# The last projection pairs product by product, the first scan items moved beside them, and a new order at five seams of a hybrid SSD block

## The chip, the cores and the metric

One Trainium2 chip, one core of it. The metric is the device time of one execution in microseconds; the time before is the median of three runs.

## What is computed

The reference is one pre-norm encoder block on a sequence of 1024 rows of 1024 numbers in float32, with a selective scan (SSD) and a gated short convolution side by side, and a SwiGLU feed-forward part behind them:

```python
h = rmsnorm(x, norm_mix_w)
u = h @ w_in                                  # 1024 x 10272
z, xbc, dt_raw, s_b, s_c, s_x, g_a, g_b = split(u)
xbc = silu(causal_depthwise_conv(xbc, ssd_conv_w) + ssd_conv_b)
y = ssd_chunked_scan(xs, softplus(dt_raw + dt_bias), -exp(a_log), bm, cm)   # 4 groups, 8 heads each
y = group_rmsnorm((y + d_skip * xs) * silu(z)) * ssd_norm_w
branch_a = y @ w_ssd_proj
branch_b = (s_b * causal_depthwise_conv(s_c * s_x, sconv_w)) @ w_sconv_proj
x = x + (sigmoid(g_a) * branch_a + sigmoid(g_b) * branch_b) @ w_o
x = x + (silu(hn @ w_gate) * (hn @ w_up)) @ w_down      # hn = rmsnorm(x, norm_ffn_w)
out = rmsnorm(x, norm_out_w)
```

## The kernel before

Every fp32 operand is split into a high and a low part, and every product is three matmuls (high by high, low by high, high by low; lines 679 to 681, and 81 to 83 for the direct tiles). A matmul is 128 x 128 by 512 columns.

**Projection.** The input projection is worked in *pairs*: two neighbouring tiles of 128 columns of w_in are one Strassen-Winograd step of seven products (class Pair, lines 834 to 908). A *slot* is one product of one pair, 12 matmuls; `slots` lists them in order, and a pair costs 84 matmuls. The first three pairs (`first`) go product by product, all three pairs at each product, so that the halves of the normalised x can be made beside them; the other 27 pairs go one after the other, seven slots each. For each product ScalarE writes the high part of a weight combination (`hi`, line 864), VectorE its low part (`lo`, line 868), and the results are added up on both engines (`ev`). `STAGES` says how many slots ahead of its product each stage is issued. `put` (line 823) splits one x-side operand (T1, T2, T3, B11, B12, B22 ...) into th (ScalarE) and tl (VectorE), line 76 and 77.

**Direct tiles and scans.** Twenty column tiles (`direct`: z tiles 12 to 15, then the 16 gate tiles) are plain products of 48 matmuls each (8 blocks of the inner dimension, two halves, three matmuls). Their weights are prepared one tile ahead (`direct_hi` on ScalarE, `direct_lo` on VectorE). Beside them the scan runs: `scans()` is a generator of 65 steps, and `direct_tile` pumps a step whenever `due` says so, evenly over the tiles. A scan item (one group, one block of 128 rows) has `part1` (transposes and score matmuls on TensorE, the decay matrix by Relu and Exp on ScalarE, the masked scores on VectorE, lines 408 to 457) and `part2` (state and output, lines 459 to 500). `prep2` makes the decay matrix of the item ahead. `norm` (line 502) is the gated group norm of a finished stretch: sums by TensorE, a square root chain of VectorE and ScalarE (lines 99 to 107, tiles gv, gr, gq), a transpose to a row (prt, line 532), a round trip through memory that spreads the row (rs_d, rbc, lines 536 and 538, issued by GpSimd), the scaling (line 543), and the operands of the next stage (line 557, written out at 558). `step_norms` advances every norm that is open, oldest first.

**Behind them** come the merge gemms, the output projection, the feed-forward units and the down projection, all as Strassen steps, with a seam where the feed-forward part gets its operands (`ffn_phase`: `first_half`, `second_half`), and a tail that norms the last rows and writes them.

The program order on every engine is written out by hand; each engine takes its instructions in that order, and a DMA stands in the order of the engine that issues it.

## Time and profile before

| | |
|---|---|
| median of 3 runs | 1910.98 us (1909.13 to 1911.13) |
| the profiled execution's own time | 1910.68 us |
| its span, first to last instruction | 1908.9 us |
| TensorE busy, matmuls | 1879.7 us (98%), 8905 recorded |
| VectorE, ScalarE, GpSimd busy | 68%, 51%, 9% |
| stages by TensorE: x and its norm; first three pairs | to 19.3; to about 76 us |
| 27 pairs | to 618.97 us |
| direct tiles with the scan | to about 952 us |
| merge, output projection, feed-forward, down projection | to 1901.6 us |
| tail | to 1908.9 us |

The profile counts an engine as busy while one of its instructions runs. The matmul records overlap: one is 0.39 us long while the next begins 0.227 us later, so the start-to-start distance is the price of a matmul. A row of the timeline gives start, duration, engine, line, operation and operands; in square brackets stands how long the engine stood idle before and what released it. The view of waits sums those idle times by engine, line and releaser.

### The profile page before, as it was taken

How to read it: one execution, taken by the hardware profiler on the slowest of the kernel's cores; microseconds unless marked ns; L12 is line 12 of the kernel's file. 1: busy time of each engine (PE TensorE's matmuls, PEld its weight loads, DVE VectorE, ACT ScalarE, POOL GpSimd, SP SyncE). 2: the span in 40 equal slices, each digit the busy share in tenths (PEclk: the TensorE clock that was granted, in tenths of full speed). 3: DMA queues.
4: the chain of work that ended last, by engine and by line, in shares of the span. 5: the costliest groups of instructions: out<-in, count | busy, mean ns of one | idle time of the engine just before them, and what ended most of it. 6: DMA issues, size and time to landing. Idle time of an engine off the chain costs nothing.

```text
span 1908.9 us, 24143 instructions
## 1 busy us (share of the span) xinstructions
PE 1879.7 (98%) x8905; PEld 1545.3 (81%) x8905; DVE 1299.4 (68%) x1688; ACT 970.6 (51%) x1541; POOL 169.7 (9%) x196
## 2 busy tenths in 40 slices
PE   7999999999999999999999999999999999999998
PEld 5688888888888888888878888887888888888886
DVE  7667878777785678889878548877444444456465
ACT  5545454444444987877665454464333333345333
POOL 1010111101100000101010000101211121100000
PEclk9999999999999999999999999999999999999999
DMA  5197999978959656778798665917988888867552
GB/s 181 48 275 173 240 230 236 240 187 226 264 149 288 223 194 219 251 250 269 261 321 311 226 208 203 229 80 171 215 193 220 195 193 192 232 257 286 190 196 110
DMA packets 341190, 411.97 MB, mean 216 GB/s; under 512 B 17384, under 2 KB 223936, under 8 KB 341072
## 3 DMA queue, kind: packets, MB, share of 16 engines
q1 hardware_dynamic: 284400, 308.59, 50.0%
q0 software_dynamic: 48608, 72.47, 20.9%
q10 hardware_dynamic: 8064, 29.36, 3.8%
q8 instruction: 70, 1.15, 0.2%
q14 instruction: 48, 0.39, 0.1%
HBM read 320.56 MB, written 143.15 MB: 243 GB/s over the span
## 4 chain that ended last, share of the span: by engine, by line
PE 92%; DVE 4%; ACT 2%; DMA 1%; issue 1%; SPq 0%; ACTq 0%; DVEq 0%
PE pb L679 5%; PE pb L680 5%; PE pb L681 5%; PE gb L679 5%; PE gb L680 5%; PE gb L681 5%; PE fb L681 4%; PE fb L679 4%; PE fb L680 4%; PE pr L81 4%; PE pr L83 4%; PE pr L82 4%; PE gd L679 4%; PE pd L679 4%; PE gd L681 4%; PE gd L680 4%
## 5 line engine op out<-in xcount | busy, mean ns | idle before, releaser
L77 DVE TENSOR_TENSOR wl<-ws,wh 128x1024 fp32r<-128x1024 f32 x77 | 94.0, 1221 | 121.6 <-ACT wh L76 121.6
L679 PE MATMUL gb<-qh,gh 128*128 128x512 f32 x432 | 169.1, 391 | 1.1 <-DVE h L1132 1.1
L680 PE MATMUL gb<-ql,gh 128*128 128x512 f32 x432 | 168.9, 391 | 0.0
L681 PE MATMUL gb<-qh,gl 128*128 128x512 f32 x432 | 168.7, 391 | 0.0
L681 PE MATMUL fb<-th,wl 128*128 128x512 f32 x352 | 137.1, 389 | 0.8 <-DVE wl L77 0.8
L679 PE MATMUL fb<-th,wh 128*128 128x512 f32 x352 | 137.1, 390 | 0.6 <-ACT wh L76 0.6
L680 PE MATMUL fb<-tl,wh 128*128 128x512 f32 x352 | 137.0, 389 | 0.0
L81 PE MATMUL pr<-th,wh 128*128 128x512 f32 x320 | 131.1, 410 | 0.0
L679 PE MATMUL gd<-qh,gh 128*128 128x512 f32 x324 | 126.0, 389 | 0.0
L680 PE MATMUL gd<-ql,gh 128*128 128x512 f32 x324 | 126.0, 389 | 0.0
L681 PE MATMUL gd<-qh,gl 128*128 128x512 f32 x324 | 126.0, 389 | 0.0
L83 PE MATMUL pr<-th,wl 128*128 128x512 f32 x320 | 125.1, 391 | 0.0
L82 PE MATMUL pr<-tl,wh 128*128 128x512 f32 x320 | 124.9, 390 | 0.0
L76 ACT ACTIVATE qh<-cb 128x1024 fp32r<-128x1024 f32 x98 | 99.8, 1018 | 38.0 <-PE gb L680 17.1
L77 DVE TENSOR_TENSOR ql<-cb,qh 128x1024 fp32r<-128x1024 f32 x98 | 115.6, 1180 | 1.6 <-ACT qh L76 1.4
L74 DVE SCALAR_TENSOR_TENSOR gl<-ca,gh 128x1024 fp32r<-128x1024 f32 (+1 forms) x60 | 70.5, 1174 | 49.0 <-ACT gh L73 49.0
L681 PE MATMUL fd<-th,wl 128*128 128x512 f32 x264 | 102.7, 389 | 0.0
L679 PE MATMUL fd<-th,wh 128*128 128x512 f32 x264 | 102.7, 389 | 0.0
L680 PE MATMUL fd<-tl,wh 128*128 128x512 f32 x264 | 102.7, 389 | 0.0
L679 PEld LDWEIGHTS gb<-qh,gh 128*128 128x128 f32 x432 | 81.5, 189 | 18.4 <-DVE h L1132 1.4
L679 PE MATMUL pb<-th,wh 128*128 128x512 f32 x240 | 94.4, 394 | 1.0 <-ACT u L894 1.0
L681 PEld LDWEIGHTS gb<-qh,gl 128*128 128x128 f32 x432 | 81.5, 189 | 17.1
(324 smaller groups left out, 4702.3 us busy)
## 6 DMA issues: line engine op xcount, KB each, us to landing
ws<-in_w_in_dram SPq DMA_DIRECT2D x80, 512.0 KB, 6.3
ws<-in_w_gate_dram SPq DMA_DIRECT2D x77, 256.0 KB, 3.9
ws<-in_w_up_dram SPq DMA_DIRECT2D x77, 256.0 KB, 4.4
ca<-u_d SPq DMA_DIRECT2D x35, 512.0 KB, 5.3
ab<-ac_d SPq DMA_DIRECT2D x32, 512.0 KB, 6.0
xbc_g<-cv ACTq DMA_DIRECT2D x24, 512.0 KB, 7.0
ws<-ws POOLq DMA_DIRECT2D x22, 512.0 KB, 6.4
wd_d<-in_w_down_dram SPq DMA_DIRECT2D x20, 512.0 KB, 10.8
```

The lines of the kernel that those rows point to most:

```text
L74: nc.vector.scalar_tensor_tensor(lo, src, -1.0, hi.bitcast(F32), op0=ALU.mult, op1=ALU.subtract)
L76: nc.scalar.activation(hi, src, AF.Copy)
L77: nc.vector.tensor_sub(lo, src, hi.bitcast(F32))
L81: nc.tensor.matmul(o, lh, rh, start=first, stop=False)
L82: nc.tensor.matmul(o, lh, rl, start=False, stop=False)
L83: nc.tensor.matmul(o, ll, rh, start=False, stop=last)
L679: nc.tensor.matmul(o, lh, rh, start=first, stop=False, skip_group_check=True)
L680: nc.tensor.matmul(o, lh, rl, start=False, stop=False, skip_group_check=True)
L681: nc.tensor.matmul(o, ll, rh, start=False, stop=last, skip_group_check=True)
```

## The change

1. Z tiles 12 to 15 become two more pairs (`z_pairs` up to 16), and `direct` holds the 16 gate tiles only.
2. The last three pairs (three z pairs) are worked product by product: n = 1, 2, 6 for all three, then n = 5 and 3 for each, then 7 for all, then 4 for all. The stage that makes the weights of product 7 is now tied to product 3, which goes before it. Weight loads of these pairs come later and closer together (`load_pairs`).
3. Six scan steps (`EARLY`) are pumped beside the last eleven slots: the loads of the first items with 10 slots left, part1 of the first three items with 6, 5 and 2 left, part2 of the first two with 3 and 0 left. One step was there before, with 2 slots left. The direct tiles pump the other steps, now over 16 tiles.
4. `step_norms` advances the newest norm first.
5. Start of the program: two of the first four x loads and the other four are issued by ScalarE instead of SyncE, the later weight loads of the first pairs by GpSimd. The operand T2 is put one step earlier.
6. Feed-forward seam: ScalarE scales one of four row blocks instead of two, the operand T3 is summed by an accumulating DMA instead of VectorE, and one of the two subtractions of T4 goes a step earlier.
7. Tail: the sum of squares goes to the square root without an add of its own (part of it is known before), and the last row block is written in two halves from two queues.

```diff
         def step_norms():
-            for n in list(norms):
+            for n in norms[::-1]:
...
-    z_pairs = [Pair(i * P, (silu_z(i), silu_z(i + 1))) for i in range(0, 12, 2)]
+    z_pairs = [Pair(i * P, (silu_z(i), silu_z(i + 1))) for i in range(0, 16, 2)]
...
-    NF = len(first)
+    NF, NL = len(first), 3
     slots = [(p, n) for n in (1, 2, 5, 6, 7, 3, 4) for p in first] + \
-        [(p, n) for p in rest_p for n in ORDER]
+        [(p, n) for p in rest_p[:-NL] for n in ORDER] + \
+        [(p, n) for n in (1, 2, 6) for p in rest_p[-NL:]] + \
+        [(p, n) for p in rest_p[-NL:] for n in (5, 3)] + \
+        [(p, n) for n in (7, 4) for p in rest_p[-NL:]]
...
-        for stage, what, d in STAGES[n]:
+        for stage, what, d in STAGES[{7: 3, 3: 7}.get(n, n) if p in rest_p[-NL:] else n]:
...
-    direct = [(wslab(w_in, i * P), z_raw(i)) for i in range(12, 16)]
+    direct = []
     for j in range(KT):
         direct += [(wslab(w_in, GA0 + j * P), gate_raw(ga_d[j])), (wslab(w_in, GB0 + j * P), gate_raw(gb_d[j]))]
...
-                due = turn[0] * SCAN_STEPS // (len(direct) * 2 * KT - 4)
+                due = turn[0] * (SCAN_STEPS - 5) // (len(direct) * 2 * KT - 4)
...
-            rows0 = h1_rows(0, (2, 3))
+            rows0 = h1_rows(0, (3,))
...
             raw0[0].clear()
+            for k in range(2):
+                nc.gpsimd.dma_start(raw1[0][k], raw1[1][k], accum_op=ALU.add)
             every(put("T2", t2))
             yield
             every(put("T1", t1))
             yield
-            for k in range(2):
-                V.tensor_add(raw1[0][k], raw1[1][k], raw1[0][k])
             every(put("T3", raw1[0]))
             yield
+            V.tensor_sub(raw0[1][0], raw0[1][0], t2[0])
             every(put("B22", raw1[1]))
             yield
-            for k in range(2):
-                V.tensor_sub(raw0[1][k], raw0[1][k], t2[k])
+            V.tensor_sub(raw0[1][1], raw0[1][1], t2[1])
             every(put("T4", raw0[1]))
...
-            r = finish(range(t, t + 1))
+            r = rstd2_of(sq[:, t, 0:1], known[:, m:m + 1])
...
-            nc.sync.dma_start(out[t * P:(t + 1) * P, :], fo[t])
+            if m < 3:
+                nc.sync.dma_start(out[t * P:(t + 1) * P, :], fo[t])
+            else:
+                nc.scalar.dma_start(out[t * P:(t + 1) * P, 512:1024], fo[t][:, 512:1024])
+                nc.sync.dma_start(out[t * P:(t + 1) * P, 0:512], fo[t][:, 0:512])
...
-    a0 = rows_sq(xt[0:4], "x", "avav")
+    a0 = rows_acc(xt[0:4], "x")
+    rows_sq_on("a", a0, "x")
+    rows_sq_on("v", a0, "x")
+    rows_sq_on("a", a0, "x")
+    more_loads(4)
+    more_loads(6)
+    small_loads()
+    first[1].y.load(nc.gpsimd)
...
-            yield
-        every(put("T2", t2))
+            if k == 7:
+                every(put("T2", t2))
+            yield
...
+    T_LAST = {12: "T2", 7: "T1", 3: "T3"}
+    EARLY = (10, 6, 5, 3, 2, 0)
...
         if left == 2:
             direct_lo(direct[0][0])
+        if left in EARLY:
             pump_scan()
```

Two places in the program show what this does to the order on the engines.

**The end of the pairs, ScalarE.** Before, from the high part for the last product (wk, its pair's product 4) to the decay matrix of the first scan item (th are the two halves of operand B12, wh a direct tile's weights, u a z tile and its silu):

```order
L864 ACTIVATE wk_4537<-ws_4295 128x512
L76 ACTIVATE th_4539<-br_4442 128x1024
L76 ACTIVATE th_4543<-br_4443 128x1024
L897 ACTIVATE u_4560<-pd_4547 128x512
L987 ACTIVATE wh_4563<-ws_4483 128x1024
L612 ACTIVATE u_4498<-u_4498 128x1024
L613 DMA z_g_120<-u_4498 128x1024
L905 ACTIVATE u_4560<-pb_4485 128x512
L612 ACTIVATE u_4560<-u_4560 128x1024
L613 DMA z_g_120<-u_4560 128x1024
L987 ACTIVATE wh_4630<-ws_4566 128x1024
L398 ACTIVATE ab_4586<-ab_4586,pac 128x128 x8
```

Now, from the silu of the last pair to B12 (the first of the three wk for product 4 stands just ahead of it):

```order
L613 ACTIVATE u_4533<-u_4533 128x1024
L614 DMA z_g_121<-u_4533 128x1024
L399 ACTIVATE ab_4689<-ab_4689,pac 128x128 x8
L401 ACT_TABLE_LOAD
L401 ACTIVATE ab_4689<-ab_4689 128x1024
L437 ACTIVATE bh_4794<-pcb_4790 128x128
```

```order
L401 ACTIVATE ab_4691<-ab_4691 128x1024
L865 ACTIVATE wk_4835<-ws_4333 128x512
L437 ACTIVATE bh_4848<-pcb_4844 128x128
L441 ACTIVATE xw_4851<-xx_4847 128x512
L455 ACTIVATE y_4779<-bc_4685,cols 128x128 x2
L455 ACTIVATE y_4780<-x_598_4687,cols 128x128 x2
L397 ACTIVATE cd_4864<-ab_4783 128x8
L399 ACTIVATE ab_4783<-ab_4783,pac 128x128 x8
L401 ACTIVATE ab_4783<-ab_4783 128x1024
L865 ACTIVATE wk_4889<-ws_4378 128x512
L76 ACTIVATE th_4891<-br_4716 128x1024
L76 ACTIVATE th_4895<-br_4717 128x1024
```

The decay matrix and part1 of the first scan items, which followed all weights of the pairs, now stand between the high parts of products 4 of the second and third pair, and B12 stands behind the last of these.

On VectorE, the same place now (tl is the low part of B12, the last two rows of wk are the low parts for products 4):

```order
L451 TENSOR_TENSOR xw_4851<-xx_4847,xw_4851 128x512
L900 TENSOR_TENSOR u_4709<-u_4709,pb_4505 128x512
L869 TENSOR_TENSOR wk_4835<-ws_4333,wk_4835 128x512
L77 TENSOR_TENSOR tl_4892<-br_4716,th_4891 128x1024
L77 TENSOR_TENSOR tl_4896<-br_4717,th_4895 128x1024
L900 TENSOR_TENSOR u_4749<-u_4749,pb_4520 128x512
L869 TENSOR_TENSOR wk_4889<-ws_4378,wk_4889 128x512
```

The low part for the last product 4 stands behind both tl, which read what ScalarE makes last.

**The last scan norms, GpSimd and VectorE.** GpSimd before, with the row's round trip (rs_d, rbc) of the norm before the last, and the operands yt of the norm before that:

```order
L558 DMA yt_d_162<-s_1240_8139 128x2x512
L558 DMA yt_d_163<-s_1241_8140 128x2x512
L558 DMA yt_d_164<-y_6768 128x2x512
L536 DMA rs_d_137<-rst_8232 4x128
L538 DMA rbc_8235<-rs_d_137 128x512
L558 DMA yt_d_165<-y_6316 128x2x512
```

and now:

```order
L559 DMA yt_d_162<-s_1250_8162 128x2x512
L559 DMA yt_d_163<-s_1251_8163 128x2x512
L537 DMA rs_d_137<-rst_8238 4x128
L539 DMA rbc_8241<-rs_d_137 128x512
L559 DMA yt_d_164<-y_6836 128x2x512
L559 DMA yt_d_165<-y_6405 128x2x512
```

The round trip no longer stands behind the third yt. On VectorE the scaling by rbc and the square root chain of the last norm (gv to gr) stood, before:

```order
L543 SCALAR_TENSOR_TENSOR y_7211<-y_7211,cols,rbc_8235 128x512 x2
L543 SCALAR_TENSOR_TENSOR y_7212<-y_7212,cols,rbc_8235 128x512 x2
L99 TENSOR_SCALAR gv_8383<-pq_8378 128x4
L102 RECIPROCAL gr_8385<-gr_8385 128x4
L104 TENSOR_TENSOR gq_8388<-gr_8385 128x4
```

and now:

```order
L544 SCALAR_TENSOR_TENSOR y_7260<-y_7260,cols,rbc_8241 128x512 x2
L99 TENSOR_SCALAR gv_8388<-pq_8383 128x4
L102 RECIPROCAL gr_8390<-gr_8390 128x4
L104 TENSOR_TENSOR gq_8393<-gr_8390 128x4
L105 TENSOR_TENSOR gq_8393<-gq_8393,gv_8388 128x4
L106 TENSOR_SCALAR gq_8393<-gq_8393 128x4
L107 TENSOR_TENSOR gr_8390<-gr_8390,gq_8393 128x4
L544 SCALAR_TENSOR_TENSOR y_7261<-y_7261,cols,rbc_8241 128x512 x2
```

The chain stands behind half of the scaling instead of all of it.

## Rows read from the trace of the kernel before

**Rows 1.** The page, busy time of TensorE and its share of the span and the other engines beside it.

```profile
PE 1879.7 (98%) x8905; PEld 1545.3 (81%) x8905; DVE 1299.4 (68%) x1688; ACT 970.6 (51%) x1541; POOL 169.7 (9%) x196
```

**Rows 2.** The waits of TensorE over the whole span: line that waited, releaser, us in total, times, longest.

```profile
PE prt L532 <- DVE gr L107: 2.1, 1, 2.1
...
PE gb L679 <- DVE h L1132: 1.1, 1, 1.1
...
PE fb L681 <- DVE wl L77: 0.8, 1, 0.8
PE fb L679 <- ACT wh L76: 0.6, 1, 0.6
```

**Rows 3.** The timeline of TensorE near its end; 13 matmuls begin between the first and the last row.

```profile
1898.27 0.39 PE L680 MATMUL gb<-ql,gh 128*128 128x512 f32 x1
...
1901.22 0.39 PE L681 MATMUL gb<-qh,gl 128*128 128x512 f32 x1
```

**Rows 4.** The timeline of TensorE at the end of the pairs: the first matmul of the first direct tile, part1 of the first scan item from its transposes to the next product, and the score products of a part2.

```profile
618.97 0.39 PE L81 MATMUL pr<-th,wh 128*128 128x512 f32 x1
...
622.37 0.38 PE L426 MATMUL pxt<-ident,bc 128*128 128x128 f32 x2
...
623.06 0.49 PE L81 MATMUL pr<-th,wh 128*128 128x512 f32 x1
...
631.57 1.09 PE L489 MATMUL pdg<-ab,xx 128*64 128x128 f32 x16
```

**Rows 5.** The timeline of ScalarE from the last pair to the second scan item: a high part of a combination, a silu with the DMA issue behind it, B12, the Relu that begins the decay matrix of the first item, and the first and last instruction of part1.

```profile
601.25 0.63 ACT L864 ACTIVATE wk<-s 128x512 fp32r<-128x512 f32 x1 [0.53 <-DVE s L847]
601.79 1.05 ACT L612 ACTIVATE u<-u 128x1024 f32<-128x1024 f32 x1
602.87 0.33 ACTq L613 DMA_DIRECT2D z_g<-u  x1
...
609.51 2.00 ACT L76 ACTIVATE th<-br 128x1024 fp32r<-128x1024 f32 x2
...
622.23 2.43 ACT L398 ACTIVATE ab<-ab,pac 128x128 f32<-128x128 f32 x8
...
626.94 0.26 ACT L436 ACTIVATE bh<-pcb 128x128 fp32r<-128x128 f32 x1
...
631.51 1.06 ACT L400 ACTIVATE ab<-ab 128x1024 f32<-128x1024 f32 x1
```

**Rows 6.** The timeline of VectorE in the same stretch: both low parts of B12, the last addition to a z tile, and an operand of 512 columns that is written as a low part is.

```profile
610.59 2.36 DVE L77 TENSOR_TENSOR tl<-br,th 128x1024 fp32r<-128x1024 f32 x2 [0.72 <-ACT th L76]
...
616.45 0.69 DVE L901 TENSOR_TENSOR u<-u,pd 128x512 f32<-128x512 f32 x1 [0.83 <-PE pd L681]
...
628.77 0.68 DVE L450 TENSOR_TENSOR xw<-xx,xw 128x512 fp32r<-128x512 f32 x1
```

**Rows 7.** Windows of the span: length, busy time of TensorE, its weight loads, VectorE, ScalarE and GpSimd (instructions), granted TensorE clock, DMA share, GB/s. The first two are direct tiles with the scan, the third lies behind the wait of prt.

```profile
800.00:900.00 100.00, 100.00 (x627) 82.57 (x626) 88.82 (x148) 79.61 (x189) 8.96 (x14) 1.00 0.81 264
900.00:950.00 50.00, 50.00 (x317) 41.50 (x316) 45.67 (x78) 31.55 (x69) 3.30 (x5) 1.00 0.75 254
985.00:990.00 5.00, 5.00 (x18) 3.95 (x18) 4.98 (x5) 2.78 (x5) 0.04 (x1) 0.74 0.98 333
```

**Rows 8.** The timeline at the last scan norms: GpSimd's third yt and the row rs_d, VectorE's scaling and the square root chain, and TensorE from prt on; 13 matmuls begin from 983.25 to 987.68, these two among them.

```profile
964.32 0.72 POOL L558 DMA_DIRECT2D yt_d<-y  x1 [2.69 <-DVE y L557]
...
965.03 0.53 POOL L536 DMA_DIRECT2D rs_d<-rst  x1
...
979.12 2.74 DVE L543 SCALAR_TENSOR_TENSOR y<-y,cols,rbc 128x512 f32<-128x512 f32 x4 [2.89 <-DMA rbc<-rs_d]
...
981.77 0.15 DVE L99 TENSOR_SCALAR gv<-pq 128x4 f32<-128x4 f32 x1
...
983.25 0.48 PE L679 MATMUL gb<-qh,gh 128*128 128x512 f32 x1
...
987.68 0.39 PE L679 MATMUL gb<-qh,gh 128*128 128x512 f32 x1
```

**Rows 9.** The waits of TensorE from 50 to 62 us, the first use of T2.

```profile
PE pb L680 <- DVE tl L77: 0.8, 1, 0.8
PE pb L679 <- ACT th L76: 0.5, 1, 0.5
```

**Rows 10.** The timeline of the feed-forward seam: ScalarE's two row blocks and VectorE's two sums for T3.

```profile
1248.41 2.19 ACT L135 ACTIVATE hn<-h,nr 128x1024 f32<-128x1024 f32 x2 [1.10 <-DVE nr L107]
...
1295.53 2.35 DVE L1205 TENSOR_TENSOR br<-br,br 128x1024 f32<-128x1024 f32 x2
```

**Rows 11.** The page, DMA issues: the transfers by which GpSimd adds one weight tile to another, KB each and us to landing.

```profile
ws<-ws POOLq DMA_DIRECT2D x22, 512.0 KB, 6.4
```

**Rows 12.** The timeline of the tail: the add of the sums of squares.

```profile
1903.25 0.16 DVE L1423 TENSOR_TENSOR fss<-sqf 128x1 f32<-128x1 f32 x1 [0.79 <-ACT fo L1405]
```

**Rows 13.** The timeline of the start: SyncE's issue of two weight loads, the square of the fourth row block, the column constants and the square root.

```profile
7.59 5.51 SPq L165 DMA_DIRECT2D ws<-in_w_in_dram  x2
...
9.86 1.23 DVE L115 SCALAR_TENSOR_TENSOR xn<-x 128x1024 f32<-128x1024 f32 x1 [3.13 <-DMA x<-in_x_dram]
...
10.70 0.32 ACT L1534 ACTIVATE cols<-pc 128x176 f32<-128x176 f32 x1 [1.14 <-PE pc L1533]
...
11.41 0.20 ACT L101 ACTIVATE nr<-nv 128x4 f32<-128x4 f32 x1 [0.39 <-DVE nv L99]
```

More of the change, by code (lines that the diff above doesn't have):

```diff
@@ L228, in hybrid_block @@
     warm = cp.tile([P, 1], F32, name="warm")
+    for i in range(4):
+        (nc.scalar if i % 2 else nc.sync).dma_start(xt[i], x[i * P:(i + 1) * P, :])
     nc.scalar.activation(warm, epst, AF.Sqrt)
-    for i in range(4):
-        nc.sync.dma_start(xt[i], x[i * P:(i + 1) * P, :])
     consts = page("c")
@@ L241, in hybrid_block, with more_loads @@
     nc.gpsimd.dma_start(rb[56:80, :], scw[0].rearrange("k (i p) -> (k i) p", p=P))
-    def more_loads():
-        for i in range(4, NT):
-            nc.sync.dma_start(xt[i], x[i * P:(i + 1) * P, :])
+    def more_loads(i):
+        for i in (i, i + 1):
+            nc.scalar.dma_start(xt[i], x[i * P:(i + 1) * P, :])
     d2 = cp.tile([16, 2], F32, name="d2")
@@ L946, in hybrid_block, with load_pairs @@
     loaded = [0]
-    def load_pairs(n):
+    def load_pairs(i):
+        n, late = (i + 11) // 7 + 1, i + 11 - 7 * (len(pairs) - NL)
+        if late > 0:
+            n = len(pairs) - NL + 1 + late // 2
         while loaded[0] < min(n, len(pairs)):
@@ L957, in slot @@
         p.ev(n)
-    z_held = []
-    def z_raw(i):
-        def f(ps, hf):
-            if hf == 0:
-                z_held.append((i, page("gt")))
-            nc.scalar.activation(z_held[-1][1][:, hf * 512:hf * 512 + 512], ps, AF.Copy)
-            if hf and len(z_held) == 2:
-                for k, t in z_held:
-                    nc.scalar.activation(t, t, AF.Silu)
-                    nc.scalar.dma_start(z_d[k], t)
-                z_held.clear()
-        return f
-    direct = [(wslab(w_in, i * P), z_raw(i)) for i in range(12, 16)]
+    direct = []
     for j in range(KT):
@@ L1405, in squares, with rstd2_of @@
             nc.scalar.activation(fo[t][:, no], h1[t][:, no], AF.Square, accum_out=sq[:, t, j:j + 1])
-        def rstd2_of(ssq, n, s):
+        def rstd2_of(ssq, b):
             shp = list(ssq.shape)
-            r = sp.tile(shp, F32, tag="rr", name=nm(s + "r"))
-            nc.scalar.activation(r, ssq, AF.Sqrt, scale=1.0 / n, bias=epst)
-            v = sp.tile(shp, F32, tag="rv", name=nm(s + "v"))
-            V.tensor_scalar(v, ssq, 1.0 / n, EPS, op0=ALU.mult, op1=ALU.add)
+            r = sp.tile(shp, F32, tag="rr", name=nm("fr"))
+            nc.scalar.activation(r, ssq, AF.Sqrt, scale=1.0 / D, bias=b)
+            v = sp.tile(shp, F32, tag="fv", name=nm("fv"))
+            V.tensor_scalar(v, ssq, 1.0 / D, b, op0=ALU.mult, op1=ALU.add)
             V.reciprocal(r, r)
-            q = sp.tile(shp, F32, tag="rq", name=nm(s + "q"))
+            q = sp.tile(shp, F32, tag="rq", name=nm("fq"))
             V.tensor_mul(q, r, r)
@@ L1497, in hybrid_block @@
     first[0].y.load()
-    more_loads()
-    for p in first[1:]:
-        p.y.load()
-    nc.sync.dma_start(wdt_s, w_in[:, DT0:DT0 + H].rearrange("(k p) f -> p k f", p=P))
-    for p in first:
-        p.x.load()
-    small_loads()
     loaded[0] = NF
@@ L1526, in steps_pe @@
                 j == len(todo) - 1 and part == 1)
-    a0 = rows_sq(xt[0:4], "x", "avav")
+    a0 = rows_acc(xt[0:4], "x")
[6 more added lines that the diff above has]
+    first[1].y.load(nc.gpsimd)
+    nc.gpsimd.dma_start(wdt_s, w_in[:, DT0:DT0 + H].rearrange("(k p) f -> p k f", p=P))
+    first[2].y.load(nc.gpsimd)
+    rows_sq_on("v", a0, "x")
     a1 = rows_acc(xt[4:8], "x")
     del xt
+    for p in first:
+        p.x.load(nc.gpsimd)
     pc = bank("pc")
@@ L1638, in hybrid_block @@
             steps_pe(1, 1)
-        load_pairs((i + 11) // 7 + 1)
+        load_pairs(i)
         if i >= 4 * NF + 2:
@@ L1663, in hybrid_block @@
         make(i)
-        load_pairs((i + 11) // 7 + 1)
+        load_pairs(i)
         pump()
@@ L1670, in hybrid_block @@
         left = n_slots - 1 - i
-        if left in (4, 3, 2):
-            del T[{4: "T2", 3: "T1", 2: "T3"}[left]]
+        if left in T_LAST:
+            del T[T_LAST[left]]
         if left == 9:
```

8 lines of the change are left out of this document (5 added, 3 removed).

## The prediction

> **What bounds the kernel now.** The page comes first. TensorE is busy 1879.7 of 1908.9 us [rows 1], so the time is its work plus about 29 us in which it does nothing; every other engine matters only where TensorE waits for it. The reader should therefore take two prices: that of a matmul, and that of each wait of TensorE. Thirteen matmuls begin in 1901.22 - 1898.27 = 2.95 us [rows 3], 0.227 us each; a slot of 12 is 2.72 us. The view of TensorE's waits gives the seams that the change touches: 2.1 us at prt, 1.1 at the feed-forward part's first operands, 0.8 and 0.6 later in that seam [rows 2]. The end of the pairs has no entry there: TensorE goes from the last pair into the direct tiles without a pause.
>
> **The change part by part.** The sum is made on the profiled execution's 1910.7 us (span 1908.9, 1.8 around it); that run lies 0.3 under the median of 1910.98, and the 0.3 is added at the end.
>
> *Z tiles.* Four direct tiles were 4 x 48 = 192 matmuls; two pairs are 2 x 84 = 168. 24 fewer at 0.227: **-5.4 us**, certain, since TensorE is full there. The added combinations on ScalarE and VectorE lie in the pairs' stage, where the view of waits shows nothing for them.
>
> *The last pairs with the scan beside them.* I follow ScalarE in the time frame of before, in which the pairs end at 618.97 [rows 4]. Two more pairs are 14 slots, and the slot with 6 left is the eighth of them: it ends at 618.97 + 8 x 2.72 = 640.7, its result at 640.9 (a record is 0.39 long, 0.23 of that in the slot). Behind it VectorE adds up the last pair's z tile (0.69 [rows 6]), ScalarE makes its silu (1.05) and issues its store (0.33) [rows 5]: 643.0. From there ScalarE has one piece of work behind another, as the order shows. The first decay matrix: from 622.23 to 626.94 in the trace, 4.7. Part1 of the first item: from 626.94 to 631.51 + 1.06, 5.6. The high part for the second pair's product 4: 0.6. Part1 of the second item: 5.6. The high part for the third pair's: 0.6. B12's two high parts: 2.0 [rows 5]. That ends at 643.0 + 19.1 = 662.1. VectorE then has the second half of tl (2.36/2 = 1.2), an addition (0.69) and the low part for the last product (0.68) in front of TensorE [rows 6]: 664.6. TensorE would want this low part at the third matmul of the last slot. It has five slots (13.6), three part1 of 623.06 - 622.37 = 0.69, and one part2 of three matmuls and 1.09 of scores (1.8) [rows 4] between 640.7 and that slot, and two matmuls: 640.7 + 13.6 + 2.1 + 1.8 + 0.5 = 658.7. So TensorE waits **+5.9 us** in all, some 1.6 of it a slot earlier (there the second item's operands on VectorE stand in front of the low part), and the rest at the last slot. Nothing absorbs this: behind it TensorE is full again. Lower end 0: if those weights were ready in time, nothing is won, because nothing was waited for before. Upper end 8: 2 more if the store issues or the loads of the first items come late.
>
> *The clock behind that wait.* The nearest row: behind the 2.1 us at prt TensorE ran partly at half clock (mean granted 0.74 from 985 to 990 [rows 7]); 12 steps took 987.68 - 983.25 = 4.43 us [rows 8] and not 2.72, so 1.7 lost. The new wait is longer: **+1.7**; ends 0 and 1.7.
>
> *Denser direct tiles.* The stage had 960 matmuls of tiles for 32 scan items, 30 per item; now 768 for 59 of 65 steps, 26 per item. Its 333 us gave 10.4 us per item, now 10.4 - 4 x 0.227 = 9.5. VectorE was busy 88.82 + 45.67 of 150 us [rows 7], 9.3 per item, and one tenth goes with the fewer tile weights: 9.2 of 9.5. That fits, so **0**, with the matmuls and the tile prepared ahead as cover; but if the cover is gone each tenth of a microsecond per item shows. Ends 0 and +11.5 (a rival).
>
> *Norms, newest first.* TensorE's prt waits for the chain gv to gr, which waits on VectorE behind four scalings of 2.74 us in all, which wait 2.89 us for rbc [rows 8]. Two things move. GpSimd issues rs_d in front of the third yt, and that yt, issued at 964.32, had waited 2.69 for VectorE; GpSimd was free from 961.6, and rs_d goes then and not at 965.0 [rows 8]: 3.4 us earlier, and rbc with it. And the chain passes two of the four scalings, 1.4. Together 4.8 us against a wait of 2.1 to 2.3, which goes, and the half clock behind it goes too: 2.3 + 1.7 = **-4.0**. Ends: -4.0, and -1.4 if rbc lands no earlier.
>
> *T2 a step earlier.* It takes away waits of 0.8 and 0.5 [rows 9]; what ScalarE does in that step instead is delayed by 2 us, and something of it is late: **-1.0**; ends -1.3 and 0.
>
> *Feed-forward seam.* ScalarE scales one row block less, 2.19/2 = 1.1 [rows 10], in front of the operand that TensorE waits 1.1 for; VectorE gets a third block instead, which runs beside it: -1.0. T3's sum takes 2.35 us of VectorE [rows 10] in front of what TensorE later waits 0.8 and 0.6 for [rows 2]. As a DMA it takes 6.4 for a tile of the same size [rows 11] and has two steps of time; one subtraction of T4 goes forward too: -1.2. Together **-2.2**; ends -2.5, and 0 if the sum lands late.
>
> *Tail.* One VectorE operation of 0.16 [rows 12] and its handover leave the chain, and the last store is half as large per queue: **-0.3**; ends 0 and -0.6.
>
> *Start.* The square of the fourth row block waits 3.13 for its rows; SyncE spent 5.51 us on issuing two loads [rows 13]. With ScalarE's queue used as well the rows may come earlier, but the constants are copied at 10.70 and the square root begins at 11.41 [rows 13], behind them on ScalarE, so not more than 0.4 can be won: **-0.4**. The four issues of later x rows now stand on ScalarE in front of both: 0.33 each [rows 5] fit into its wait for rows, but two held up as SyncE's two were cost 5.5. Ends -0.5 and +5.5; I take the former's side, since ScalarE's queue holds two transfers where SyncE's had nine. The Trainium skill, DMA: Bandwidth & Descriptors, section Issuing engines are not separate DMA queues, says that transfers of all issuers run on the same 16 engines, and only issue time is saved. By that rule the rows come when they came before, the term is 0 and the sum 1905.7; no row here shows the two queues together.
>
> Sum: -5.4 + 5.9 + 1.7 - 4.0 - 1.0 - 2.2 - 0.3 - 0.4 = -5.7. 1910.7 - 5.7 + 0.3 = **1905.3 us**.
>
> **The rivals.**
>
> *No wait at the end of the pairs.* If the weights of the last products are ready (the ScalarE instructions run faster in a row than each row shows, or TensorE is behind for another reason), 5.9 + 1.7 drop out: 1897.7. For it: no wait stood there before. Against it: 19 us of ScalarE's work, one after another, for 18 us of TensorE's, and VectorE's 2.5 behind it.
>
> *VectorE becomes the bound beside the direct tiles: slower.* Of 10.4 us per item VectorE was idle 1.07 from 800 to 950 [rows 7]. If that idleness is waits for ScalarE and TensorE inside each item, which a shorter period does not remove, an item takes 9.2 + 1.07 = 10.3 and not 9.5: 0.8 for each of the 14.4 items of that stretch, +11.5: 1917. For it: VectorE is at 97% of the new period. Against it: before, it idled because it was not needed sooner. It ends slower only when at least 0.95 of the 1.07 stay (9.5 us more); with half of it, 0.24 for 14.4 items, 3.5 more, it ends at about 1909.
>
> *The row's round trip is no earlier.* The change would not do there what its order says: DMA share is 0.98 behind the seam [rows 7], and rbc may land when traffic lets it. Then -1.4 and not -4.0: 1907.9.
>
> **How the numbers follow.** A measurement of this kernel can tell 0.2%, 3.8 us, from no change; the limits are 1907.2 and 1914.8. My forecast has 0.48 (its own range 1902.5 to 1908, and four fifths of that lie under 1907.2), the rival without the wait 0.20, the late round trip 0.13 (two fifths faster), half of VectorE's idleness 0.08 (no change), VectorE as the bound 0.11 (slower). Faster: 0.38 + 0.20 + 0.05 = 0.63. Within 0.2%: 0.10 + 0.08 + 0.08 = 0.26. Slower: 0.11. The range leaves out the last case and the outer tenth: 1897 to 1911.
>
> **What would show it.** Right: 24 fewer matmuls of the projection; in the view of waits a new entry of TensorE's pb products for VectorE's wk of about 6 us in the last two slots, with ScalarE busy without a gap for 19 us ahead of it, and a stretch of half clock behind it; the prt entry gone, and the clock whole there; the entries of the feed-forward seam under 0.5 together. Wrong: no such entry at the end of the pairs (the first rival); entries of pxt, pst or pr for VectorE all through the direct tiles (the second); prt still waiting for gr about 1 us, with rbc landing when it did (the third). A start that lasts longer than 19.3 us to the first projection product would show the last term wrong.

## The result, and the profile after

The changed kernel takes 1913.08 us (median of 21 runs, 1911.20 to 1914.52), the kernel before 1909.23 (21 runs, 1908.02 to 1912.06): ratio 1.0018, 95% interval 1.0012 to 1.0025. The change costs 3.9 us where 5.7 less were forecast, and the time lies above the range. The profiled execution of the changed kernel took 1914.05 us with a span of 1912.3; before it was 1910.68 and 1908.9. Single executions of 2352, 8446 and 3845 us (of e5_b12late, e9_b12early and e12_four below) are left out of all medians.

The page after has 24 matmuls fewer and nearly the same busy time of TensorE [rows 1]:

```profile
PE 1878.5 (98%) x8881; PEld 1541.8 (81%) x8881; DVE 1310.6 (69%) x1704; ACT 971.1 (51%) x1546; POOL 177.3 (9%) x204
```

TensorE's waits over the whole span, the lines that matter here (us in total, times, longest), answer to [rows 2]:

```profile
PE pb L680 <- DVE u L900: 5.0, 2, 3.9
PE pd L680 <- ACT u L898: 4.3, 3, 2.5
...
PE fb L682 <- DVE wl L77: 0.5, 1, 0.5
PE prt L533 <- DVE gr L107: 0.4, 1, 0.4
PE poff L476 <- DVE st L485: 0.4, 1, 0.4
```

The entry of the feed-forward part's first operands is gone, prt and fb are small, and two entries are new, both at the end of the pairs. One of them, pb for VectorE, the forecast had; the other, pd for ScalarE, it had not. The timeline of TensorE shows where they fall:

```profile
626.00 0.39 PE L682 MATMUL pd<-th,wk 128*128 128x512 f32 x1
627.51 0.50 PE L680 MATMUL pd<-th,wh 128*128 128x512 f32 x1 [1.12 <-ACT u L898]
...
635.74 0.50 PE L680 MATMUL pd<-th,wh 128*128 128x512 f32 x1 [2.46 <-ACT u L898]
...
643.81 0.50 PE L680 MATMUL pd<-th,wh 128*128 128x512 f32 x1 [0.69 <-ACT u L898]
...
663.08 0.47 PE L680 MATMUL pb<-th,wk 128*128 128x512 f32 x1 [1.07 <-DVE u L900]
...
665.76 0.39 PE L682 MATMUL pb<-th,wk 128*128 128x512 f32 x1
670.05 0.47 PE L680 MATMUL pb<-th,wk 128*128 128x512 f32 x1 [3.90 <-DVE u L900]
```

The first row is the last matmul of a product 5, the second the first of the product 3 that goes on in the same bank: 1.51 us between them and not 0.23. Measured from start to start beyond what the step takes without a wait (0.227 us, and 0.03 behind the short transposes ahead of 663.08), the three waits for ScalarE are 1.28, 2.62 and 0.85 us (4.8 together), the two for VectorE 1.31 and 4.06 (5.4). ScalarE beside the first kind:

```profile
626.88 0.58 ACT L898 ACTIVATE u<-pd 128x512 f32<-128x512 f32 x1
...
633.11 0.63 ACT L865 ACTIVATE wk<-ws 128x512 fp32r<-128x512 f32 x1 [3.67 <-DVE ws L850]
633.65 1.04 ACT L613 ACTIVATE u<-u 128x1024 f32<-128x1024 f32 x1
634.72 0.33 ACTq L614 DMA_DIRECT2D z_g<-u  x1
635.09 0.60 ACT L898 ACTIVATE u<-pd 128x512 f32<-128x512 f32 x1 [0.40 <-ACT u L613]
...
649.05 2.45 ACT L399 ACTIVATE ab<-ab,pac 128x128 f32<-128x128 f32 x8 [0.40 <-ACT u L613]
...
665.88 1.99 ACT L76 ACTIVATE th<-br 128x1024 fp32r<-128x1024 f32 x2
```

At 635.09 the copy of product 5 out of its bank stands behind a high part that had waited 3.67 us for VectorE, and behind a silu and a store. From 649.05 the chain of the forecast runs: it ends with B12 at 667.87, 18.8 us later, where 19.1 had been added up. VectorE behind it:

```profile
666.95 2.36 DVE L77 TENSOR_TENSOR tl<-br,th 128x1024 fp32r<-128x1024 f32 x2 [3.41 <-ACT th L76]
669.23 0.68 DVE L900 TENSOR_TENSOR u<-u,pb 128x512 f32<-128x512 f32 x1
```

The addition that empties the bank of product 7 follows tl, and the last product 4 begins when it is done. Windows of the changed kernel (columns as in [rows 7]):

```profile
637.00:641.00 4.00, 4.00 (x12) 3.13 (x11) 0.97 (x2) 0.25 (x1) 0.00 (x0) 0.57 0.49 131
...
671.00:675.00 4.00, 4.00 (x15) 3.26 (x13) 4.00 (x8) 3.45 (x9) 0.00 (x0) 0.57 0.38 155
800.00:900.00 100.00, 100.00 (x636) 82.77 (x635) 95.44 (x167) 82.09 (x196) 9.94 (x15) 1.00 0.80 258
900.00:950.00 50.00, 50.00 (x327) 41.02 (x326) 48.71 (x81) 41.83 (x99) 4.56 (x7) 1.00 0.84 280
```

Behind either group of waits the granted clock of this execution falls to half, the lower of its two levels, for 3.4 us (the windows of 4 us show 0.57 in the mean), which is 1.7 us of work each time. In the direct tiles VectorE is busy 95.4% and 97.4%, where it was 88.8% and 91.3% [rows 7], and TensorE is not idle in either window.

The last scan norms, in answer to [rows 8]:

```profile
971.77 0.71 POOL L559 DMA_DIRECT2D yt_d<-s  x1 [9.65 <-DVE s L558]
972.47 0.53 POOL L537 DMA_DIRECT2D rs_d<-rst  x1
...
981.86 0.59 POOL L539 DMA_DIRECT2D rbc<-rs_d  x1 [8.86 <-PE gd L682]
...
987.31 1.42 DVE L544 SCALAR_TENSOR_TENSOR y<-y,cols,rbc 128x512 f32<-128x512 f32 x2 [2.50 <-DMA rbc<-rs_d]
988.64 0.16 DVE L99 TENSOR_SCALAR gv<-pq 128x4 f32<-128x4 f32 x1
...
990.09 0.27 PE L533 MATMUL prt<-ident,gr 128*4 128x128 f32 x1 [0.42 <-DVE gr L107]
```

prt waits 0.4 us in place of 2.1, the clock stays whole, and the chain gv to gr stands behind two scalings.

### The profile page after: what moved, and what is told of

It reads as the page before. It is cut to its first block, busy times and chain, and to the rows that moved or that the text cites. A ratio compares the mean times of both kernels' runs of the same rounds, so it can differ in the third digit from the quotient of the medians.

```text
span 1912.3 us, 24119 instructions
## 1 busy us (share of the span) xinstructions
PE 1878.5 (98%) x8881; PEld 1541.8 (81%) x8881; DVE 1310.6 (69%) x1704; ACT 971.1 (51%) x1546; POOL 177.3 (9%) x204
## 4 chain that ended last, share of the span: by engine, by line
PE 85%; DVE 6%; ACT 4%; DMA 2%; issue 2%; ACTq 0%; POOL 0%; SPq 0%; DVEq 0%; POOLq 0%
PE pb L680 5%; PE pb L681 5%; PE pb L682 5%; PE gb L680 5%; PE gb L681 5%; PE gb L682 5%; PE fb L682 4%; PE fb L680 4%; PE fb L681 4%; PE pd L680 4%; PE pd L681 4%; PE pd L682 4%; PE gd L681 3%; PE gd L680 3%; PE gd L682 3%; PE fd L680 3%
## 5 line engine op out<-in xcount | busy, mean ns | idle before, releaser
L81 PE MATMUL pr<-th,wh 128*128 128x512 f32 x256 | 105.9, 414 | 0.0
L680 PE MATMUL pb<-th,wk 128*128 128x512 f32 x256 | 100.5, 393 | 5.2 <-DVE u L900 5.0
L680 PE MATMUL pd<-th,wh 128*128 128x512 f32 x256 | 100.8, 394 | 4.3 <-ACT u L898 4.3
L680 PE MATMUL pb<-th,wh 128*128 128x512 f32 x256 | 101.0, 394 | 0.5 <-ACT u L895 0.5
L681 PE MATMUL pb<-tl,wh 128*128 128x512 f32 x256 | 100.0, 391 | 0.9 <-DVE tl L77 0.8
L682 PE MATMUL pb<-th,wk 128*128 128x512 f32 x256 | 100.6, 393 | 0.2 <-DVE wk L869 0.2
```

The source lines that it names most:

```text
L81: nc.tensor.matmul(o, lh, rh, start=first, stop=False)
L680: nc.tensor.matmul(o, lh, rh, start=first, stop=False, skip_group_check=True)
L681: nc.tensor.matmul(o, lh, rl, start=False, stop=False, skip_group_check=True)
L682: nc.tensor.matmul(o, ll, rh, start=False, stop=last, skip_group_check=True)
```

## The experiments

Each kernel but e8_all53 was timed with five rounds beside the kernel before; intervals are at 95%. The kernel before came to 1909.03 to 1909.35 us in every group of runs, so the medians can be set against each other.

**e1_apart.** Products 5 and 3 of the last three pairs set apart.

```diff
-        [(p, n) for p in rest_p[-NL:] for n in (5, 3)] + \
+        [(rest_p[k - NL], n) for k, n in ((0, 5), (1, 5), (0, 3), (2, 5), (1, 3), (2, 3))] + \
```

> The changed kernel, but in the last three pairs product 3 of a pair no longer follows its product 5 directly: the order is 5, 5, 3, 5, 3, 3 over the three pairs, so another pair's product lies between. Theory (product 3 goes on in the PSUM bank of product 5 and must wait for ScalarE's copy of it; that wait and the half clock behind it are time of their own): TensorE's pd waits for u of 4.3 us go, and with them the half clock of 3.4 us length near 637: 4.8 + 1.7 = 6.5 us less than the change, about 1906.6; the waits of pb for VectorE (5.0) stay. Rival (ScalarE and VectorE have too much to do at the end of the pairs, and a wait removed comes back at the next product): the pb waits grow by about as much, the time stays within 1.5 us of 1913.1.

1906.93 us, ratio 0.9987 (0.9979 to 0.9996), 6.2 less than the change. TensorE's waits from 610 to 675 us are one entry:

```profile
PE pb L680 <- DVE u L900: 5.0, 2, 3.9
```

The pd waits are gone, no half clock is granted before 664, and the pb waits are what they were. The theory holds: with another product in between the copy is out in time, so what stood in the way was the bank handed over side by side and not ScalarE's load as a whole.

**e8_all53.** The same neighbourhood put into every later pair of the kernel before (one run, no interval).

```diff
-        [(p, n) for p in rest_p for n in ORDER]
+        [(p, n) for p in rest_p for n in (1, 2, 6, 5, 3, 7, 4)]
...
-        for stage, what, d in STAGES[n]:
+        for stage, what, d in STAGES[{7: 3, 3: 7}.get(n, n) if p not in first else n]:
...
-        if left in (4, 3, 2):
-            del T[{4: "T2", 3: "T1", 2: "T3"}[left]]
+        if left in (4, 3, 1):
+            del T[{4: "T2", 3: "T1", 1: "T3"}[left]]
```

> The kernel before with product 3 directly behind product 5 in each of the 27 later pairs (order 1, 2, 6, 5, 3, 7, 4), the weights of 7 and 3 tied to the one that goes first; nothing else. Theory (the bank of product 5 is handed over through ScalarE's copy, whatever else ScalarE does): 27 waits of pd for ScalarE's u of 0.7 us or more each, 19 us or more in all: 1928 or more. Rival (the waits in the changed kernel came from ScalarE's lateness in the last three pairs alone): fewer than 8 us of such waits, under 1918.

1974.14 us. The two largest waits of TensorE:

```profile
PE pd L679 <- ACT u L897: 25.3, 27, 2.3
PE pb L679 <- DVE u L899: 22.3, 27, 0.9
```

The theory holds: 27 waits for ScalarE, though it has no scan beside it there. In 21 of them ScalarE begins the copy 0.04 us after product 5 ends, and they are 0.69 us long; in six the copy begins later, they are 0.74 to 2.3 long and bring the mean to 0.94. And 27 more that I had not expected, since the same order puts product 4 directly behind product 7, and product 4 waits for VectorE's addition of 7 out of its bank: 0.83 us each in the mean. The pairs end 63.2 us later, 3.4 of it lost to half clock (two stretches), so a handover costs (63.2 - 3.4) / 54 = 1.1 us of TensorE's time from start to start.

**e2_noearly.** The changed kernel without scan items beside the pairs.

```diff
-    EARLY = (10, 6, 5, 3, 2, 0)
+    EARLY = (2,)
...
-                due = turn[0] * (SCAN_STEPS - 5) // (len(direct) * 2 * KT - 4)
+                due = turn[0] * SCAN_STEPS // (len(direct) * 2 * KT - 4)
```

> The changed kernel, but with no scan items beside the last slots: one step with 2 slots left, as before the change, and the other 64 spread over the 16 direct tiles. Theory (the scan items on ScalarE hold up the additions and low parts that the last products 4 wait for): the pb waits of 5.0 us and the half clock near 671 go, the pd waits near 626 to 643 stay, as no scan work is there yet: 5.4 + 1.7 = 7 us less than the change, about 1906. Rival (VectorE is the bound beside the direct tiles, and the early items relieve it): new waits of pxt, pst, poff or pr for VectorE in the direct tiles, together 5 us or more, and the time is 1911 or more.

1922.97 us, ratio 1.0068 (1.0056 to 1.0081). The pb waits go and the pd waits stay (4.2), as the theory had it, but 9.9 us slower than the change: poff waits 3.7 us for ScalarE's and 3.0 for VectorE's state, prt 1.5, and the clock is half for 13.6 us in three stretches. TensorE's waits from 610 to 1000 us begin:

```profile
PE pd L680 <- ACT u L898: 4.2, 3, 2.5
PE poff L476 <- ACT st L483: 3.7, 2, 3.3
PE poff L476 <- DVE st L485: 3.0, 1, 3.0
```

The rival was right about the direct tiles. None of the three half-clock stretches lies behind the pd waits (they begin at 897, 955 and 989 us), though these waits are as long as in the changed kernel.

**e3_zpairs.** The kernel before with the two z pairs alone, in the old order.

```diff
-    z_pairs = [Pair(i * P, (silu_z(i), silu_z(i + 1))) for i in range(0, 12, 2)]
+    z_pairs = [Pair(i * P, (silu_z(i), silu_z(i + 1))) for i in range(0, 16, 2)]
...
-    direct = [(wslab(w_in, i * P), z_raw(i)) for i in range(12, 16)]
+    direct = []
```

> The kernel before with one part of the change: z tiles 12 to 15 as two more pairs, in the old order (seven products of one pair after another), 16 direct tiles with all the scan steps of before beside them; nothing else is changed. Theory (the 24 matmuls are won in full, what lost time is the new order of the last three pairs): no new waits at the end of the pairs, 5.4 us less than before, about 1903.8. Rival (the shorter stretch of direct tiles is bound by VectorE): waits for VectorE there eat 3 us or more of it, 1907 or more.

1925.24 us, ratio 1.0085 (1.0071 to 1.0098): 24 matmuls fewer and 16 us slower. TensorE's waits from 880 to 1000 us, and a window:

```profile
PE pq L527 <- DVE mc L1038: 5.6, 1, 5.6
PE poff L475 <- DVE st L484: 5.4, 1, 5.4
PE prt L532 <- DVE gr L107: 3.1, 2, 2.6
PE poff L475 <- ACT st L482: 2.3, 1, 2.3
```

```profile
800.00:900.00 100.00, 97.16 (x630) 79.32 (x629) 96.76 (x167) 83.14 (x204) 11.57 (x18) 1.00 0.79 262
```

The rival was right about place and sign, and it cost far more than the 3 us it had named. VectorE is 96.8% busy in this window; the scan falls behind the tiles and its last items and norms are waited for, with the clock at half for 17 us in two stretches. That VectorE's load alone makes the scan late is not shown: ahead of the 5.4 us wait, which ends at 950.4, VectorE works without a gap from 942.2 us on, but just before that it stood idle for 3.2 us until ScalarE had a merge operand (gh).

**e4_seams.** Norms newest first, T2 a step earlier and the feed-forward seam in the kernel before (those lines of the diff and no others).

> The kernel before with three of the change's seams alone: norms newest first, T2 a step earlier, the feed-forward seam. From the trace of the changed kernel: prt's wait 2.1 less 0.4 and the half clock behind it 1.7, T2 about 1.0, the feed-forward seam 2.0: about 6.4 us less than before, 1902.8. If these were won only because the rest of the change had moved things in time, less than half of it: 1906 or more.

1904.38 us, ratio 0.9973 (0.9964 to 0.9983): 4.7 less by the medians, 6.0 by the spans of the profiled executions, in which prt, the first operands of the feed-forward part and its fb for ScalarE no longer appear. The seams are won without the rest of the change. (Why medians and spans differ here is told below, with the half clock.)

**e5_b12late.** e1_apart with B12 split behind the last weights.

```diff
-        if left == 4:
-            every(put("B12", b12))
...
         if left == 2:
             direct_lo(direct[0][0])
+        if left == 1:
+            every(put("B12", b12))
```

> The kernel with products 5 and 3 apart (e1_apart), and operand B12 split with 1 slot left instead of 4, so that its two th and tl stand behind the additions and weights of the last product 4, not in front. Theory (the wait of 4.1 us before the last product is for VectorE's addition, which stands behind tl and so behind ScalarE's th and everything ahead of that): this wait goes, the 1.3 us at the second product 4 stays (its addition stands behind part1 of the second item), the half clock goes with it: 4.1 + 1.7 less than e1_apart, about 1901.1. Rival (ScalarE and VectorE are simply late by then): the first direct tile waits instead, for its weights or for B12, 3 us or more, and the time is 1905 or more.

1910.58 us, ratio 1.0005 (0.9996 to 1.0014), 3.7 more than e1_apart. TensorE's waits from 600 to 690 us:

```profile
PE pr L81 <- ACT th L76: 3.7, 1, 3.7
PE poff L476 <- DVE st L485: 1.8, 1, 1.8
PE pb L680 <- DVE u L900: 1.1, 1, 1.1
PE pr L82 <- DVE tl L77: 0.8, 1, 0.8
```

My theory fell and the rival held: the 4.1 us moved to the first direct tile, which needs B12, and grew. ScalarE was late, not badly ordered.

**e6_free.** The same, with part1 of the second item a slot later (EARLY is 10, 6, 4, 3, 2, 0).

> As e5_b12late, and part1 of the second scan item with 4 slots left instead of 5, behind the addition of the second pair's product 7. Theory: the last 1.3 us of waits at the end of the pairs go too, about 1899.8; no wait of pb over 0.5 us after 600. Rival: the later scan item is missed at the end of the direct tiles, where poff or prt wait 1 us or more, and the time is that of e5_b12late or above.

1911.99 us, ratio 1.0014 (1.0005 to 1.0023). No pb wait is left, and pr waits 5.2 us for th: moved once more, the same reason.

**e9_b12early.** e1_apart with B12 loaded with 11 slots left and split with 7 left, in front of ScalarE's backlog.

```diff
-        if left == 9:
+        if left == 11:
             b12 = [page("br", HB) for _ in range(2)]
...
-        if left == 4:
+        if left == 7:
             every(put("B12", b12))
```

> The kernel with products 5 and 3 apart (e1_apart), and operand B12 loaded with 11 slots left and split with 7 left, ahead of the first scan item on ScalarE, not behind the second. Theory (what TensorE waits for at the last product 4 is ScalarE's backlog from the first scan item on; only work that goes into ScalarE's idle time ahead of it is a gain): th of 2.0 us lies in ScalarE's gaps before the first decay matrix, the wait before the last product falls by 2 to 4 us and no new wait comes in the direct tiles: 1903 to 1905. Rival (the memory pages for it are free only later, so the split waits and holds up ScalarE): a wait of the same size a few slots earlier, 1906 or more.

1905.59 us, ratio 0.9980 (0.9971 to 0.9989), 1.3 less than e1_apart. The pb wait falls from 5.0 to 1.2 and the clock is whole, but pst waits 1.6 (two waits) and poff 1.3 that did not before. Of the 7.1 us that the two pb waits and the half clock had cost, 1.3 were won: the wait fell as the theory said, but new ones came, and the time lies between the theory's 1905 and the rival's 1906.

**e7_pairwise.** The changed kernel, early items kept, but the last three pairs one after another, with the old STAGES and the old places of the deletions.

```diff
-        [(p, n) for p in rest_p[:-NL] for n in ORDER] + \
-        [(p, n) for n in (1, 2, 6) for p in rest_p[-NL:]] + \
-        [(p, n) for p in rest_p[-NL:] for n in (5, 3)] + \
-        [(p, n) for n in (7, 4) for p in rest_p[-NL:]]
+        [(p, n) for p in rest_p for n in ORDER]
...
```

> The changed kernel with the last three pairs one after another, seven products each in the old order, and all else kept, the six early scan steps with them. Theory (the order product by product is what leaves room for the early items, since it makes most weights before them): the last pair's products wait for weights that stand behind the scan items on ScalarE, 8 us or more, and the time is 1913 or more. Rival (the order gives nothing, the early steps alone keep the direct tiles fed): no pd waits, pb waits of 6 us or less, 1907 or less.

1907.70 us, ratio 0.9992 (0.9983 to 1.0001), 5.4 less than the change and 0.8 more than e1_apart. Waits from 600 to 675 us:

```profile
PE pb L680 <- ACT u L895: 4.6, 1, 4.6
PE pd L682 <- DVE wk L869: 2.4, 1, 2.4
```

The theory (8 us or more) was too high; the rival's 1907 was nearer, though a pd wait came that it had denied. Product by product with 5 and 3 apart is 0.8 us better than this order, less than the intervals tell apart; as the change has it, it is 5.4 worse.

**e11_three and e12_four.** e7_pairwise with three (5, 2, 0) and four (8, 4, 2, 0) early steps, and the other steps spread accordingly.

> As e7_pairwise (the change with the last three pairs one after another), but with three scan steps beside the last slots instead of six: the loads with 5 slots left, part1 of the first item with 2 and of the second with 0 left. Theory (each early item costs TensorE some us of waiting for ScalarE at the end of the pairs, each one that is missing costs waits for the scan at the end of the 16 direct tiles): waits at the end of the pairs under 3 us instead of 7, but 3 to 8 us of waits of poff, prt or pq after 880; 1905 to 1912, no clear gain over e7_pairwise (1907.7). Rival (the optimum lies between none and six): 1904 or less.

> As e11_three with four steps: the loads with 8 slots left, part1 of the first two items with 4 and 2 left, part2 of the first with 0. Theory: waits of 3 to 6 us at the end of the pairs and 0 to 4 after 880, 1904 to 1910. Rival (a middle number keeps both ends covered): waits under 3 us in all, 1903 or less.

1912.90 us, ratio 1.0023 (1.0014 to 1.0031), and 1911.98, ratio 1.0015 (1.0006 to 1.0024): no optimum between, and both above what the theory had allowed. With three, poff waits 7.8 us (one of them 4.9 at the first items) and prt 1.5; with four, one single pd wait for ScalarE's copy of product 5 is 7.0 us: part1 had come in front of that copy.

**e10_onepair.** e4_seams and one of the two z pairs: 18 direct tiles, 12 matmuls fewer, old order, no early items.

```diff
-    z_pairs = [Pair(i * P, (silu_z(i), silu_z(i + 1))) for i in range(0, 12, 2)]
+    z_pairs = [Pair(i * P, (silu_z(i), silu_z(i + 1))) for i in range(0, 14, 2)]
...
-    direct = [(wslab(w_in, i * P), z_raw(i)) for i in range(12, 16)]
+    direct = [(wslab(w_in, i * P), z_raw(i)) for i in range(14, 16)]
```

> The three seams of e4_seams, and one of the two new z pairs: z tiles 12 and 13 as a pair in the old order, z tiles 14 and 15 and the 16 gates as 18 direct tiles with all scan steps of before. 12 matmuls fewer are 2.7 us. Theory (with 20 direct tiles the scan was just covered, with 16 it was late by 13 us; what tiles are taken away beyond the cover comes back as waits for the scan): with 18 the waits for st, gr or wl in the direct tiles are some 3 to 6 us, so 1904 to 1908, no gain over e4_seams. Rival (the cover gives out between 18 and 16): no such waits over 1.5 us, 1901.7.

1902.50 us, ratio 0.9965 (0.9951 to 0.9978): the fastest version, 6.5 less than the kernel before beside it (1909.04) and 10.6 less than the change. TensorE's waits from 600 to 1000 us and a window:

```profile
PE poff L475 <- ACT st L482: 0.7, 1, 0.7
PE prt L532 <- DVE gr L107: 0.3, 1, 0.3
```

```profile
800.00:900.00 100.00, 100.00 (x638) 82.08 (x637) 93.46 (x157) 81.85 (x198) 11.04 (x17) 1.00 0.83 272
```

The rival was right: 18 tiles still cover the scan. None of the kernels with 16 direct tiles comes under e4_seams (1904.38); the best of them, e9_b12early, has 1905.59 (all but e3_zpairs carry the new start and tail as well).

## Why the prediction was wrong

The forecast summed to -5.7 on the profiled execution; its span grew by 3.4. From start to start on TensorE, term by term:

| term | forecast | measured |
|---|---|---|
| 24 matmuls fewer | -5.4 | -5.4 |
| product 3 behind product 5 in one bank | not seen | +4.8 |
| half clock behind that | not seen | +1.7 |
| products 4 behind the scan items | +5.9 | +5.4 |
| half clock behind that | +1.7 | +1.7 |
| denser direct tiles | 0 | +0.6 |
| norms newest first, with the clock | -4.0 | -3.4 |
| T2 (first three pairs) | -1.0 | -0.6 |
| feed-forward seam | -2.2 | -2.2 |
| tail | -0.3 | +0.1 |
| start (to the first product's second matmul) | -0.4 | +0.2 |

The measured terms come to 2.9; the remaining 0.5 of the span I did not place. Besides, the forecast was made against a median of 1910.98 from three runs, and 21 runs give 1909.23.

**The half-clock rows** hold for this pair of profiled executions and not for every execution. Of the 27 executions of the kernel before that were timed beside e5 to e8, nine have a mean granted clock of 0.998 and a median of 1910.69 us, 18 have 0.999 and 1908.90; the profiled one, with 3.4 us at half clock behind prt, has 0.998 and 1910.68. Of the changed kernel's 21, seven have 0.997 (median 1913.58, the profiled one among them) and 13 have 0.998 (1912.01). The steps of 1.8 and 1.6 us are near the price of one stretch, 1.7. So most executions of the kernel before seem not to have had the half clock behind prt at all, and the forecast's 1.7 for it was read from one of the third that had; this would also be why e4_seams wins 6.0 by the spans and 4.7 by the medians. It is argued from the mean clocks, since only one execution of each kernel has a trace. The traces agree in that e2_noearly has the same pd waits with no half clock behind them, and e8_all53 has it behind two of its four waits of over 2 us.

**The step that failed** is in the terms of the z tiles and of the last pairs: the new order of the products was put at nothing, because the added work of the pairs would lie where TensorE waits for nothing. It was read from the old order, where another product (7) lies between 5 and 3, and 3 between 7 and 4. I followed the weights of the new order through ScalarE and VectorE, and not the banks. Product 5 starts a bank, ScalarE copies it out, and product 3 goes on adding in the same bank; side by side, TensorE has to wait for the copy. The waits cost 4.8 us and the half clock behind them 1.7, and no term stood for them. e1_apart takes this away alone and gives back 7.1 us by the spans, of the 9.1 that lie between forecast and measurement there, and 6.2 by the medians. e8_all53 shows 0.69 us per such wait where nothing else stands in front of the copy, as does the third wait of the changed kernel (643.81, idle 0.69); so about 2.1 of the 4.3 us of the pd entry are the handover itself, and the rest is what stood in front of the first two copies on ScalarE.

**The end of the pairs** was sized right: 5.9 against 5.4, the chain on ScalarE 19.1 against 18.8, and the half clock behind it. One detail was off: what releases TensorE is VectorE's addition out of the bank of product 7 (done at 669.91); the low part that the forecast had in its place is done 0.6 us later, just ahead of the third matmul, which needs it. e5_b12late and e6_free show that this wait is ScalarE's backlog and moves with the order.

**Denser direct tiles: right as a sum, for a reason that I had not seen.** I gave 0 because VectorE would be busy 9.2 of 9.5 us per item, and it ran at 95 to 97% with one wait of 0.4 us at the end of the stage. But without the early items it does not hold: e2_noearly loses 10 us against the change, e3_zpairs 16 against before. So something like the rival of VectorE as the bound exists, its place was right, and the early items are what keeps it off; the busy share does not tell the two cases apart (95.4% without a wait in the changed kernel's window, 96.8% with waits in e3_zpairs), and whether VectorE's load or the order of the work is behind it stays open. So the -5.4, which the forecast calls certain, was not: with 16 tiles it is paid for either at the end of the pairs (e1_apart, e7_pairwise) or at the end of the tiles (e3_zpairs); only the first 12 matmuls are free (e10_onepair: 1.9 us under e4_seams, 2.7 forecast).

**The feed-forward seam** came as worked out.

**The norms: right in size, in part by luck.** The forecast had the row's round trip 3.4 us earlier. Counted from the transpose prt of the norm before (958.00 before, 966.58 now), rs_d went 1.1 us earlier and rbc was there 0.4 earlier. Newest first also puts two products of the newest norm (L514) in front of the second yt's sum on VectorE, so that yt, issued at 971.77, and rs_d behind it came later than the forecast's 961.6 would be in this frame (970.2); and from rs_d to rbc's issue passed 9.4 us, against 7.2 before. So the third rival was right about the round trip. What won the term is that the chain passes two scalings (1.3 us) and that the 0.4 us wait left over has no half clock behind it, which that rival's -1.4 had not counted.

**T2.** Its own waits fell from 1.64 us to 0.41 from start to start, as forecast, but a wait for the low part tl at product 7 (75.3 us) grew from 0.43 to 0.96. (The first three pairs end at about 100 us; at 76, as the table ahead has it, they are only at product 7.)

**Tail.** From the last matmul to the end of the span are 7.69 to 7.70 us in all five kernels with the old tail and 7.81 to 7.96 in nine with the new one. The chain is 0.3 shorter to the last scaling, but the span ends 4.1 us behind the issue of the two halves, where it was 3.5 behind the one whole store; what fills the difference stays open.

**Start.** In the profiled execution the square root began 1.0 us earlier than before (10.37 against 11.41 [rows 13]) and the first product 0.7 later (19.98 against 19.33). Of the 0.7 little counts, because before the change the first product's second matmul had to wait:

```profile
20.41 0.50 PE L680 MATMUL pb<-tl,wh 128*128 128x512 f32 x1 [0.61 <-DVE tl L77]
```

Now it begins at 20.56 without a wait, so the term is +0.2. Over all kernels the first product comes at 18.2 to 20.6 us with the new start (nine) and 17.2 to 19.4 with the old (five), the square root at 10.3 to 10.6 and 10.1 to 11.4; no gain can be shown. Why none reached the first product stands at the end. The rule of the Trainium skill that spreading transfers over issuers saves only issue time (DMA: Bandwidth & Descriptors, section Issuing engines are not separate DMA queues) gave 0 for this term. No run decides between it and my term: the last of the first four row blocks landed at 8.6 to 8.7 us with the new start and at 8.5 to 9.8 with the old.

## What to carry to other kernels

When a change reorders products, follow the accumulator banks as well as the operands: for each product ask who must read the bank before it, on which engine, and what stands in front of that read; two products of one bank side by side cost about 1.1 us of TensorE's time here, and more when other work stands in front of the read. A stage that lives as cover for another (here the tiles for the scan) is not shortened for free: find by steps how much of it is spare (two of four tiles here) before counting its matmuls as gain. And look at the granted clock of several executions before a half-clock stretch of the one with a trace goes into a sum. Where an engine is late by its load, moving one of its pieces moves the wait; only work put into its idle time ahead helps, and most of that came back too.

## What the runs showed of the hardware that was not expected

VectorE's first six row scalings take 2.47 us in all five kernels with the old start. In the nine with the new start, in which GpSimd issues weight loads at the same time, they take 3.26 to 4.62; one scaling takes 0.48 us in the old kernels and up to 0.95 in the new ones. The timeline of the changed kernel:

```profile
10.37 0.20 ACT L101 ACTIVATE nr<-nv 128x4 f32<-128x4 f32 x1
...
11.60 4.62 DVE L137 TENSOR_SCALAR xn<-x,nr 128x512 f32<-128x512 f32 x6
12.05 3.54 POOL L165 DMA_DIRECT2D ws<-in_w_in_dram  x4
```

and of the kernel before:

```profile
9.76 0.99 POOL L255 DMA_DIRECT2D al<-in_a_log_dram  x2 [0.29 <-DMA c<-in_norm_ffn_w_dram]
...
12.66 2.47 DVE L137 TENSOR_SCALAR xn<-x,nr 128x512 f32<-128x512 f32 x6
```

The transposes wait for these rows, and the time won at the square root is gone by then: from the square root to the first product pass 7.1 to 8.4 us with the old start, 7.9 to 9.5 in the six kernels whose scalings take 3.26 to 3.48, and 9.6 to 10.1 in the three whose scalings take 4.31 to 4.62. No kernel changed the issuer alone, so that GpSimd's issuing slows VectorE is the nearest explanation and not shown by itself. Also, the last stores of 256 KB landed 2.5 to 2.9 us after their issue in the nine kernels with the new tail, those of 512 KB after 2.6: halving them bought nothing.
